# Halo rows as column strips, interleaved feature groups and re-timed DMA in a hybrid decoder layer on eight cores

## The chip, the cores and the metric

The program runs on all 8 cores of one Trainium2 chip (two dies of four cores); every core executes the same instructions on its own part of the data. In the profiles of this kernel TensorE does the matrix products, VectorE, ScalarE and GpSimd the rest of the arithmetic, and SyncE only issues DMAs. The metric is the time of the slowest core in microseconds (us). Such a program has a second, slower state in some executions, in which the cores of one die show a lower granted TensorE clock (0.91 on one die and 0.98 on the other in an execution of 1988.9 us, for example); only executions in the fast state are compared here. A profile covers one execution, with all eight cores; where I give "the median of the cores", it is over the eight cores of one profiled execution.

## The reference, cut to what matters

```python
def mixer(xn, conf_buf, lru_buf, h0, p, reset_first):
    proj = xn @ p['w_in']                                  # 2048 -> a_val, a_gate, b_x, b_gate (1024 each)
    a_val, a_gate, b_x, b_gate = jnp.split(proj, ...)
    u = a_val * jax.nn.sigmoid(a_gate)
    ca, new_conf = causal_dwconv(u, conf_buf, ...)         # depthwise, 31 taps
    ca = silu(layer_norm(ca, ...))
    xc, new_lru = causal_dwconv(b_x, lru_buf, ...)         # depthwise, 4 taps
    h, h_last = rglru(xc, h0, ...)                         # gates, then a linear scan over time
    cb = h * gelu(b_gate)
    return jnp.concatenate([ca, cb], axis=-1) @ p['w_out'], ...

def conv_ffn(xn, buf, p):
    up = xn @ p['w_up']                                    # 2048 -> 12288
    upc, new_buf = causal_dwconv(up, buf, ...)             # depthwise, 3 taps
    g, v = jnp.split(upc, 2, axis=-1)
    return (gelu(g) * v) @ p['w_down'], new_buf            # 6144 -> 2048

def layer(x, ...):
    x = x + rms_norm(mixer(rms_norm(x, ...))[0], ...)
    return x + rms_norm(conv_ffn(rms_norm(x, ...))[0], ...)
```

There are 4 prompts of 2048 tokens and 128 short sequences of 8 tokens. A core takes half a prompt (1024 tokens) and 16 short sequences (128 tokens): 9 tiles of 128 rows. A core with a second half also computes what the scan and the convolutions need of the first half, among that two rows just ahead of its first tile, which only the 3-tap convolution of the channel mixer reads. These two rows are the **halo tile**.

## The kernel before

The kernel writes one list of instructions per engine and derives the semaphore waits from what each reads and writes; a buffer placed over an older one waits for the older one's last readers. Each engine executes its list in order, and a DMA is issued from an engine's list, so a DMA that has to wait holds whatever stands behind it on that engine. `load("sp", ...)` is a DMA issued from SyncE, `load("pool", ...)` one from GpSimd. TensorE's products land in the banks of the PSUM memory (`PS`), from which ScalarE or VectorE copies them out.

Its stages in order are: normalise and transpose 17 row tiles, input projection and 31-tap convolutions (to about 430 us); the recurrent group with the layer norm (to about 580); output projection and the two norms, tile by tile (to about 750); up projection and down projection, in two halves of the hidden features (to about 1906); the last outputs. In the lines of the profile, xnp is a transposed row tile of the first half, which the input projection reads; xcpb the result of the 4-tap convolution of the first half, which the gates read; wab and wxb the gates' weights; ge one half of the up projection's result; hm the product that the down projection reads; a number behind a name only tells buffers apart. These parts matter for the argument:

```python
# diagonals for the 31-tap convolution as a matmul: built on GpSimd
def conv_prep(j):
    load("pool", r_w, T[f"ubf{j % 2}"][:, 1056:1536], st_conf_d[:, j]...)
    S.op("pool", lambda e: e.tensor_tensor(dg[:], identb..., vecs..., ALU.mult), ...)

# five transfers just ahead of the convolutions, in the stretch in which row tiles are loaded
load("pool", r_su, T["wab"][:], wa_d, ...);  load("pool", r_su, T["wxb"][:], wx_d, ...)
load("sp", r_su, T["slruc"][:], ...);        load("sp", r_su, T["slruh"][:], ...)
load("sp", r_out, s_conf_d[:, :, 0:22, :], st_conf_d[:, :, 8:30, :], [], [])

# output projection: ten tiles, the first with the 2 halo rows
tiles = [(1022, 2, 0, None)] + [(1024 + 128 * t, 128, 2 + 128 * t, 128 * t) for t in range(9)]

# down projection, second half of the hidden features (g == 1): 36 items (feature group fg, tile)
items = [(fg, tt_) for fg in range(4) for tt_ in range(9)]
def down_load(i):
    load("sp", r_ld, T["prv"][:, i % 3, :], f_scr[rows, ...], ...)   # first half's partial sum
    if fg == 3:
        load("sp", r_x, T[f"hh{tt_ % 3}"][:], h_scr[rows, :], ...)   # h, for the residual
for i, (fg, tt_) in enumerate(items):
    down_load(i + 2)
    down_mm(g, fg, tt_, b)                                           # 24 matmuls
    tt(f, out, prv, ALU.add);  act(Square, accum);  tt(f, f, grow3, ALU.mult)
    if fg == 3:                                                      # tile complete
        ...                                                          # reciprocal root of the sum of squares
        stt(hh, f3, r, hh, ...)                                      # hh = f * r * gain + h
        load("sp", r_out, y_d[rows, :], hh[:], [kh_], [])            # output
```

Of the kernel before, what the change touches and what calls it, by code (L numbers as in the profile page):

```python
# [55 lines left out]
class Sched:  # L56
# [135 lines left out]
    "xnp0": 0, "x2_0": 0, "xna0": 15872, "xna1": 34816, "catA5": 8192, "xn20": 10528, "wp9": 0, "ca6": 53760, "f36":  # L192
    4096, "xcb0": 0, "catB2": 58400, "ca1": 58400, "ca5": 63040, "f35": 10240, "hm1": 28992, "hm16": 31296, "xs2":
    53760, "grow2": 28992, "ca3": 67680, "hh2": 16384, "wp6": 33600, "catB4": 60736, "catA6": 63072, "ones": 72320,
    "catB7": 37184, "og1": 4096, "x2_1": 39520, "wp11": 37696, "xcpbZ": 72832, "wo03": 65408, "catB0": 73600,
    "catB3": 75936, "wu1": 78272, "wp10": 41792, "wu2": 82368, "hh0": 45888, "ve0": 45888, "grow3": 54080, "A3":
    86464, "catA3": 86464, "t3_1": 10528, "xnp1": 91104, "ca7": 106976, "flags": 111616, "hm13": 62272, "xcpZ":
    111648, "wo10": 47712, "th": 72832, "catA2": 88800, "wu4": 115616, "grow1": 78272, "wo12": 91136, "wo01":
    111648, "wo11": 99328, "wo02": 119840, "ubf1": 111648, "ge1": 50656, "ca4": 119712, "hm6": 64576, "xt1": 63040,
    "hm2": 66880, "wo13": 128032, "catA4": 136224, "wu0": 124352, "xs0": 106976, "prv": 69184, "ffnf": 69184,  # L200
    "hm15": 82240, "wp3": 107520, "ge0": 55424, "gbg1": 138560, "wu3": 128448, "f34": 75328, "slruc": 143200, "wxb":
    144736, "hm23": 84544, "hm9": 86848, "hm5": 89152, "fl": 24576, "hm18": 91456, "xcb1": 146784, "gbg2": 2464,
    "hm19": 93760, "wp5": 96064, "ca2": 132544, "hm0": 100160, "t2_0": 149248, "hm8": 102464, "xs1": 119712, "f30":
    111648, "hm4": 104768, "p1Z": 137184, "catA1": 154176, "catB1": 156512, "wo00": 158848, "hm20": 117792, "xn21":
    167040, "xcpb": 141152, "catA0": 185504, "wp2": 138560, "slruh": 167040, "us1": 77568, "f31": 120096, "catB5":
    187840, "catA7": 190176, "hh1": 126240, "xt2": 132544, "xs2_1": 143200, "dj": 134432, "hm22": 135456, "xc0":
    91136, "ov1": 111648, "hstf": 167552, "xs2_0": 147296, "wp8": 151392, "hm12": 155488, "xt0": 146784, "og0":
    120096, "ht": 192512, "hm11": 157792, "t2_1": 168096, "wp0": 200704, "f37": 142656, "bxp": 146784, "diag1":
    154976, "btl": 173024, "wu5": 162912, "p1": 150784, "t3_0": 173120, "hm7": 160096, "bxe": 96064, "t1_1": 178048,
    "ov0": 124832, "hm21": 162400, "p3Z": 154752, "wab": 182976, "hP": 185024, "hm17": 164704, "grow0": 167552,  # L210
    "wp7": 185504, "ssf": 28672, "wp1": 204800, "us0": 114976, "xcp": 168096, "catB6": 55904, "xc1": 192512, "tiny":
    208896, "t1_0": 197440, "ca0": 178048, "hm14": 189600, "sq": 185056, "ve1": 129568, "wp4": 191904, "bxpZ":
    158720, "gbg0": 202368, "ubf0": 189792, "cv": 209152, "f33": 167008, "f32": 173152, "hm10": 196000, "p3":
    173120, "dstg": 142656, "identb": 209280, "A3b": 193120, "vecs": 209536, "rs": 101024, "diag0": 197760, "f38":
    179296, "lrucf": 207008, "mu": 187840, "hm3": 198304,
# [3 lines left out]
def build_program():  # L219
# [22 lines left out]
    st_ffn_d = din("st_ffn", [128, 96, 32])  # L242

# [5 lines left out]
    ffn_d = dout("ffn", [128, 96, 34])  # L249
# [4 lines left out]
    with ExitStack() as es:  # L254
# [29 lines left out]
            ("grow1", [D], F_, 17, 20), ("grow2", [D], F_, 17, 20),  # L284
            ("ht", [D], F_, 18.2, 20), 
            ("grow3", [D], F_, 22.9, 24),
            ("ffnf", [96, 34], F_, 20, 22.9), 
# [8 lines left out]
        for i in range(2):  # L296
            BUFS += [(f"diag{i}", [31, 128], B_, 0, 8), (f"ubf{i}", [1664], B_, 0, 8), (f"us{i}", [158], F_, 0, 8.2)]
            BUFS += [(f"xc{i}", [1232], F_, 8.6 + i * 1.4, 17 + i), (f"xcb{i}", [1232], B_, 8.6 + i * 1.4, 17 + i)]
            BUFS += [(f"{t}_{i}", [1232], F_, 10 + i, 18 + 0.4 * i) for t in ("t1", "t2", "t3")]
            BUFS += [(f"x2_{i}", [D], F_, 17, 20), (f"xs2_{i}", [D], B_, 18.2, 20.5)]  # L300
            BUFS += [(f"ge{i}", [1186], F_, 20, 22.9), (f"ve{i}", [1186], F_, 20, 22.9)]
            BUFS += [(f"og{i}", [1184], F_, 20, 22.9), (f"ov{i}", [1184], F_, 20, 22.9)]
# [4 lines left out]
        for i in range(24):  # L307
            BUFS += [(f"hm{i}", [1152], B_, 20, 24)]
# [9 lines left out]
        for i in range(12):  # L318
            BUFS += [(f"wp{i}", [2048], B_, 19 if i < 4 else 20, 24)]
# [195 lines left out]
        def conv_prep(j):  # L515
            load("pool", r_w, T[f"ubf{j % 2}"][:, 1056:1536], st_conf_d[:, j].rearrange("p t s -> p (t s)"),
                 [], [(f"ubf{j % 2}", "o")])
            dg = T[f"diag{j % 2}"]
            S.op("pool", lambda e: e.tensor_tensor(
                dg[:], identb[:].unsqueeze(1).broadcast_to([128, 31, 128]),  # L520
                vecs[:, V_CW + 31 * j:V_CW + 31 * j + 31].unsqueeze(2).broadcast_to([128, 31, 128]), ALU.mult),
                ["identb", "vecs"], [(f"diag{j % 2}",)])
# [243 lines left out]
        load_w(4, after=[("xt2",)])  # L766
        p0_norm(0)
# [25 lines left out]
        conv_prep(0)  # L793
        conv_prep(1)
# [11 lines left out]
        load("pool", r_su, T["wab"][:], wa_d, [], ["wab"])  # L806
        load("pool", r_su, T["wxb"][:], wx_d, [], ["wxb"])
        load("sp", r_su, T["slruc"][:], st_lruc_d, [], ["slruc"])
        load("sp", r_su, T["slruh"][:], st_h_d.rearrange("p j s o -> p j (s o)"), [], ["slruh"])
        load("sp", r_out, s_conf_d[:, :, 0:22, :], st_conf_d[:, :, 8:30, :], [], [])  # L810
# [25 lines left out]
        for j in range(2, 8):  # L836
            conv_prep(j)
            i = j - 1
            bg = triple()
# [72 lines left out]
        tiles = [(1022, 2, 0, None)] + [(1024 + 128 * t, 128, 2 + 128 * t, 128 * t) for t in range(9)]  # L912
        NT = len(tiles)

        def p2_load(ti):
            r0, M, a0, hr = tiles[ti]
            load("sp", r_x, T[f"x2_{ti % 2}"][0:M, :], xall[r0:r0 + M, :], [], [(f"x2_{ti % 2}",)])

        def cat(k, a0, M):
            return T[f"catA{k}" if k < 8 else f"catB{k - 8}"][:, a0:a0 + M]  # L920
# [3 lines left out]

        def p2_mm(ti, k0, k1, half=None):
            r0, M, a0, hr = tiles[ti]
            b0 = 4 * (ti % 2)
            for fg in range(4):
                if fg == 2 and half is not None:
                    half()  # L930
                for k in range(k0, k1):
                    mm(PS[0:M, 512 * (b0 + fg):512 * (b0 + fg) + 512], cat(k, a0, M), T[f"wo{k // 8}{fg}"][:, k % 8, :],
                       k == 0, k == 15, cat_keys(k) + [(f"wo{k // 8}{fg}",)], PK(b0 + fg), skip=True)

        def p2_begin():
            load("sp", r_su, T["grow1"][:], grows_d[1:2, :].partition_broadcast(128), [], ["grow1"])
            load("sp", r_su, T["grow2"][:], grows_d[2:3, :].partition_broadcast(128), [], ["grow2"])
            p2_load(0)
            p2_load(1)

# [38 lines left out]
        for k0, k1 in ((0, 8), (8, 14)):  # L979
            for ti in range(2):  # L980
# [16 lines left out]
        def p2_norm(ti, between=None):  # L997
            r0, M, a0, hr = tiles[ti]
            b0 = 4 * (ti % 2)
            x2, xs, ht = T[f"x2_{ti % 2}"], T[f"xs2_{ti % 2}"], T["ht"]  # L1000
            kx, ks = (f"x2_{ti % 2}",), (f"xs2_{ti % 2}",)
            o = PS[0:M, 512 * b0:512 * b0 + 2048]
            c = tiny[0:M, 16 + 8 * (ti % 2):24 + 8 * (ti % 2)]
            kt = lambda n: ("tiny", "p2", ti % 2, n)
            act(xs[0:M, 0:1024], o[:, 0:1024], AF.Square, PK(b0, 2), [ks, kt(0)], accum=c[:, 0:1])
            if between is not None:
                between()
            act(xs[0:M, 1024:2048], o[:, 1024:2048], AF.Square, PK(b0 + 2, 2), [ks, kt(1)], accum=c[:, 1:2])
# [3 lines left out]
            stt(ht[0:M, :], o, c[:, 3:4], T["grow1"][0:M, :], ALU.mult, ALU.mult, PK(b0, 4) + [kt(3), "grow1"], ["ht"])  # L1012
            tt(x2[0:M, :], x2[0:M, :], ht[0:M, :], ALU.add, [kx, "ht"], [kx])
            if hr is not None:
                load("sp", r_st, h_scr[hr:hr + 128, :], x2[:], [kx], [("h_scr", hr)])
            act(xs[0:M, :], x2[0:M, :], AF.Square, [kx], [ks, kt(4)], accum=c[:, 4:5])
            act(c[:, 5:6], c[:, 4:5], AF.Ln, [kt(4)], [kt(5)], scale=1.0 / D, bias=EPS)
            act(c[:, 6:7], c[:, 5:6], AF.Exp, [kt(5)], [kt(6)], scale=-0.5)
            if hr is None:
                ts(c[:, 6:7], c[:, 6:7], flags[0:M, 0:1], None, ALU.mult, None, [kt(6), "flags"], [kt(6)])  # L1020
            stt(xs[0:M, :], x2[0:M, :], c[:, 6:7], T["grow2"][0:M, :], ALU.mult, ALU.mult, [kx, kt(6), "grow2"], [ks])

        def p2_turn(ti, b0):
            r0, M, a0, hr = tiles[ti]
            xs, ks = T[f"xs2_{ti % 2}"], (f"xs2_{ti % 2}",)
            for kh in range(2):
                b = b0 + kh
                pb = PS[:, 512 * b:512 * b + 512].bitcast(BF16)
                for j in range(8):
                    k = 8 * kh + j  # L1030
                    S.op("pe", lambda e, pb=pb, j=j, k=k: e.transpose(pb[:, 128 * j:128 * j + M],  # L1031
                                                                      xs[0:M, 128 * k:128 * k + 128], identb[0:M, 0:M]),
                         [ks, "identb"], PK(b))
                pv = pb.rearrange("p (j t) -> p j t", t=128)
                evac("dve" if kh == 0 else "act", T[f"xn2{kh}"][:, :, a0:a0 + M], pv[:, :, 0:M], PK(b), [(f"xn2{kh}", ti)])
# [3 lines left out]
        p2_mm(1, 15, 16)  # L1039
        p2_load(2)  # L1040
        p2_norm(1)
# [272 lines left out]
```

## Time and profile before

The fast executions of the first measurement took 1946.76 and 1948.91 us; the others (2071.99 and 3807.41) were in the slow state, and they are why the median is 2072. The table cuts the profiled execution of the kernel before at points that are easy to find in any trace (first start of an instruction on a tile), each as the median of the cores, with their spread.

| Stretch | us before | over the cores |
|---|---|---|
| start to the last gate sigmoid of the convolution stage (ScalarE on p1Z) | 430.4 | 427.0 to 433.8 |
| to the issue of the last output weight ("recurrent stage") | 147.7 | 147.0 to 147.9 |
| to the first normalising multiply of the output projection | 46.2 | 45.8 to 47.2 |
| to the last of them ("output projection") | 126.3 | 125.7 to 126.4 |
| to TensorE's end (up and down projection) | 1152.4 | 1149.0 to 1155.4 |
| TensorE's end to the kernel's end ("the end") | 36.7 | 35.2 to 38.2 |

A stretch is read on its own: a stage in which TensorE is 100% busy is shortened, at the same clock, only by less TensorE work, and one in which it stands by whatever it stands for. The lines of the profile that carry this are in the prediction. Two more views of the kernel before are needed later: what VectorE waits for in the last 80 us, and the longest wait of SyncE's list from 1780 us on. Columns of the waits: total us, times, longest.

```profile
DVE sb_hh_96 L364 <- DMA sb_hh_96<-h_scr: 7.9, 2, 4.0
DVE sb_hh_92 L364 <- DMA sb_hh_92<-h_scr: 5.8, 2, 3.8
```

### The profile page before, as it was taken

The numbers are of one execution on the slowest core, as the hardware profiler recorded it, in microseconds if no ns is written. First come the engines' busy times: TensorE is split into PE (matmuls) and PEld (weight loads), VectorE is DVE, ScalarE is ACT, GpSimd is POOL, SyncE is SP. The second block draws the span as 40 slices with busy tenths as digits, with TensorE's granted clock in tenths as the row PEclk, the third lists the DMA queues.
The fourth block names the chain that finished last, engine by engine and source line by source line (L and its number), as shares of the span: only waits on it lengthen the run. The fifth ranks groups of instructions, "written<-read, shape, count | busy, mean of one in ns | idle before, by whom it ended". The sixth has DMA issues, their size and how long they took to land.

```text
span 1944.6 us, 33585 instructions; the slowest of 8 cores (1931.5 to 1944.6 us)
## 1 busy us (share of the span) xinstructions
PE 1773.5 (91%) x10412; PEld 916.8 (47%) x10412; DVE 1012.2 (52%) x968; ACT 567.2 (29%) x1009; POOL 182.6 (9%) x247
## 2 busy tenths in 40 slices
PE   2868999999986999799999989999999999989992
PEld 2744565554442444355555544444555555544440
DVE  5534655557883554666666650001666666642243
ACT  3633234347882433222222211111222222211110
POOL 3002221101221001000000000000000000000000
PEclk9979999999998999899999999999999999999996
DMA  8672322313268435743344325556344334445566
GB/s 195 201 165 38 51 38 39 53 33 63 44 133 155 152 130 143 134 72 66 66 67 74 67 55 110 124 114 119 67 72 70 66 66 68 74 121 115 119 206 233
DMA packets 53127, 193.48 MB, mean 99 GB/s; under 512 B 6994, under 2 KB 10578, under 8 KB 44498
## 3 DMA queue, kind: packets, MB, share of 16 engines
q0 software_dynamic: 29232, 106.41, 32.6%
q1 hardware_dynamic: 23716, 84.92, 13.1%
q8 instruction: 84, 1.38, 0.3%
q14 instruction: 95, 0.78, 0.1%
HBM read 266.79 MB, written 32.35 MB: 154 GB/s over the span
## 4 chain that ended last, share of the span: by engine, by line
PE 83%; DMA 9%; DVE 4%; ACT 2%; issue 2%; SPq 0%; DVEq 0%; ACTq 0%; POOL 0%; POOLq 0%
PE ps L370 82%; DMA sb_xt_90<-xall 2%; DMA sb_wo_201<-w_out 2%; DMA sb_ffnf<-st_ffn 1%; DMA y<-sb_hh_96 1%; DMA y<-sb_hh_92 1%; DVE sb_xs_95 L364 1%; DMA sb_xt_94<-xall 1%; PE ps L463 1%; DMA y<-sb_hh_88 0%; ACT L337 0%; PE ps L1031 0%; DVE sb_btl L343 0%; DMA sb_hh_96<-h_scr 0%; SPq L373 0%
## 5 line engine op out<-in xcount | busy, mean ns | idle before, releaser
L343 DVE COPY sb_ve_108<-ps 128x1026 f32<-128x1026 f32 (+1 forms) x48 | 36.4, 800 | 306.5 <-PE ps L370 306.5
L343 DVE COPY sb_ve_122<-ps 128x1026 f32<-128x1026 f32 (+1 forms) x48 | 36.4, 800 | 108.7 <-PE ps L370 108.7
L364 DVE SCALAR_TENSOR_TENSOR sb_ov_110<-sb_ve_108,sb_vecs,sb_ov_110 128x1184 f32<-128x1184 f32 x48 | 69.7, 1451 | 5.3 <-DVE sb_ov_110 L361 0.5
L364 DVE SCALAR_TENSOR_TENSOR sb_og_109<-sb_ge_107,sb_vecs,sb_og_109 128x1184 f32<-128x1184 f32 x48 | 69.7, 1451 | 5.3 <-DVE sb_og_109 L361 0.5
L364 DVE SCALAR_TENSOR_TENSOR sb_og_123<-sb_ge_121,sb_vecs,sb_og_123 128x1184 f32<-128x1184 f32 x48 | 69.7, 1452 | 5.0
L364 DVE SCALAR_TENSOR_TENSOR sb_ov_124<-sb_ve_122,sb_vecs,sb_ov_124 128x1184 f32<-128x1184 f32 x48 | 69.7, 1451 | 5.0
L335 ACT COPY sb_dstg<-ps 128x512 f32<-128x512 f32 x36 | 21.1, 586 | 167.0 <-PE ps L370 167.0
L370 PE MATMUL ps<-sb_ubf_112,sb_diag_111 128*128 128x342 bf16 (+1 forms) x496 | 63.9, 290 | 0.0
L370 PE MATMUL ps<-sb_ubf_98,sb_diag_97 128*128 128x342 bf16 (+1 forms) x496 | 62.2, 286 | 0.0
L335 ACT COPY sb_ffnf<-sb_ve_122 128x32 f32<-128x32 f32 (+1 forms) x48 | 7.5, 205 | 178.4 <-DVE sb_ve_122 L343 178.4
L335 ACT COPY sb_ffnf<-sb_ve_108 128x32 f32<-128x32 f32 (+1 forms) x48 | 7.6, 204 | 175.3 <-DVE sb_ve_108 L343 175.2
L370 PEld LDWEIGHTS ps<-sb_ubf_112,sb_diag_111 128*128 128x128 bf16 x496 | 43.8, 99 | 19.5
L337 ACT ACTIVATE sb_og_123<-sb_og_123 128x1184 f32<-128x1184 f32 x24 | 28.6, 1191 | 82.4 <-DVE sb_og_123 L364 82.4
L337 ACT ACT_TABLE_LOAD x37 | 47.5, 1283 | 17.5 <-PE ps L370 7.8
L370 PEld LDWEIGHTS ps<-sb_ubf_98,sb_diag_97 128*128 128x128 bf16 x496 | 43.1, 97 | 18.5
L337 ACT ACTIVATE sb_og_109<-sb_og_109 128x1184 f32<-128x1184 f32 x24 | 28.6, 1190 | 79.5 <-DVE sb_og_109 L364 79.5
L370 PE MATMUL ps<-sb_xn_127,sb_wp_206 128*128 128x512 bf16 (+1 forms) x192 | 36.8, 335 | 11.8 <-ACT sb_ge_121 L335 11.8
L343 DVE COPY sb_btl<-sb_bxp 128x3 f32<-128x3 f32 x7 | 36.4, 5204 | 16.2 <-ACT sb_bxp L335 16.2
L335 ACT COPY sb_ge_107<-ps 128x1026 f32<-128x1026 f32 (+1 forms) x48 | 31.4, 705 | 34.8 <-PE ps L370 34.8
L370 PE MATMUL ps<-sb_xna_125,sb_wu_182 128*128 128x512 bf16 (+2 forms) x184 | 33.9, 330 | 6.8 <-DMA sb_wu_182<-w_in 6.8
L335 ACT COPY sb_ge_121<-ps 128x1026 f32<-128x1026 f32 (+1 forms) x48 | 31.4, 707 | 26.7 <-PE ps L370 26.7
L370 PE MATMUL ps<-sb_xn_130,sb_wp_206 128*128 128x512 bf16 (+1 forms) x192 | 36.4, 333 | 0.0
(654 smaller groups left out, 4135.7 us busy)
## 6 DMA issues: line engine op xcount, KB each, us to landing
f_scr<-sb_dstg SPq DMA_DIRECT2D x36, 256.0 KB, 3.4
sb_prv<-f_scr SPq DMA_DIRECT2D x36, 256.0 KB, 4.5
sb_xt_86<-xall SPq DMA_DIRECT2D x6, 1024.0 KB, 7.5
sb_xt_90<-xall SPq DMA_DIRECT2D x6, 1024.0 KB, 8.6
sb_xt_94<-xall SPq DMA_DIRECT2D x5, 1024.0 KB, 11.8
sb_x_1_119<-xall SPq DMA_DIRECT2D x5, 1024.0 KB, 5.4
h_scr<-sb_x_1_119 SPq DMA_DIRECT2D x5, 1024.0 KB, 3.9
sb_wp_202<-w_up POOLq DMA_DIRECT2D x8, 512.0 KB, 6.8
```

The lines of the kernel that those rows point to most:

```text
L335: S.op("act", lambda e: e.copy(out=out, in_=in_), reads, writes)
L337: S.op("act", lambda e: e.activation(out=out, in_=in_, func=func, scale=scale, bias=bias), reads, writes)
L343: S.op("dve", lambda e: e.tensor_copy(out, in_), reads, writes)
L364: S.op("dve", lambda e: e.scalar_tensor_tensor(out, a, s, b, op0, op1), reads, writes)
L370: S.op("pe", lambda e: e.matmul(out, lhsT, rhs, start=start, stop=stop, skip_group_check=skip), reads, writes)
L463: S.op("pe", lambda e, pb=pb, j=j, k=k: e.transpose(pb[:, 128 * j:128 * j + 128], xs[:, 128 * k:128 * k + 128], identb[:]), [ks, "identb"] ...
```

## The change

Its intent is to take waits of TensorE away at six places. The diff, cut to its core (left out are the new addresses of all buffers, the renamed state tensors, the exchanged order of the first two tiles of the output projection, the small operations on the halo rows, and the reloads of h for tiles 0 to 2, which now leave at item 18 of 36):

```diff
+        def conv_diag(j):                                    # now on VectorE
+            tt(T[f"diag{j % 2}"][:], identb..., vecs..., ALU.mult, ...)
@@ the five transfers go from ahead of the convolutions into their loop
+            if j == 2:    load wab, wxb
+            elif j == 4:  load slruc, slruh
+            elif j == 5:  load s_conf
@@ output projection: 9 full tiles; the halo rows in four 32-column strips of the array
-        tiles = [(1022, 2, 0, None)] + [...]
+        def halo_mm(b):
+            for k in range(16):
+                for fg in range(4):
+                    mm(PS[32 * fg:32 * fg + 32, 512 * b:512 * b + 512], cat(k, 0, 32), T[f"wo{k // 8}{fg}"][:, k % 8, :], ...)
+            act(zh[:], PS[:, 512 * b:512 * b + 512], ...)
@@ grow1, grow2, x tiles wait for the last output weight
+            last = [("wo13",)]
+            load("sp", r_su, T["grow1"][:], ..., last, ["grow1"])
@@ state of the up projection: one contiguous tile, loaded at the end of the last tile
+                load("sp", r_su, T["ffo"][:], st_ffn_d, [], [("ffo", "old")])
@@ down projection: 23 of 24 products of three tiles ahead of the last hidden group
+                if i == 0:
+                    for t in range(3):
+                        down_mm(g, fg, t, (b + t) % 8, 0, 23)
@@ last two feature groups interleaved, output in two pieces, reload right behind it
+            if g == 1:
+                items = items[:24]
+                for t in range(3):
+                    items += [(3, t), (2, 6 + t)]
+                items += [(3, t) for t in range(3, 9)]
-                load("sp", r_out, y_d[rows, :], hh[:], [kh_], [])
+                load("sp", r_out, y_d[rows, 0:1536], hh[:, 0:1536], [(kh_, 0)], [])
+                load("sp", r_out, y_d[rows, 1536:2048], hh[:, 1536:2048], [(kh_, 1)], [])
+                if tt_ < 6:
+                    hh_load(tt_ + 3)
```

## The prediction

> **What bounds the kernel now.** I read the clocks of the cores first: spans 1931.5 to 1944.6 us, clocks 0.963 to 0.966 on both dies, so the profiled execution is a fast one (its time was 1946.3 us; 1946.8 is the lowest of the timed ones, and the median of 2072 holds slow ones). All that follows is about fast executions. Next, the busy shares on the page and the stretches of time:
>
> ```profile
> PE 1773.5 (91%) x10412; PEld 916.8 (47%) x10412; DVE 1012.2 (52%) x968; ACT 567.2 (29%) x1009; POOL 182.6 (9%) x247
> ```
> ```profile
> 98.00:132.00 34.00, 15.12 (x155) 11.61 (x154) 8.76 (x8) 9.33 (x15) 0.00 (x0) 0.77 0.93 204
> ...
> 580.00:614.00 34.00, 22.25 (x81) 7.44 (x78) 16.26 (x20) 12.92 (x13) 6.29 (x11) 0.79 1.01 193
> ...
> 646.00:760.00 114.00, 114.00 (x638) 55.71 (x637) 62.76 (x41) 46.50 (x89) 0.70 (x2) 1.00 0.36 137
> 760.00:796.00 36.00, 23.43 (x166) 12.68 (x164) 11.53 (x10) 7.79 (x17) 5.63 (x11) 0.90 1.00 191
> ...
> 1865.00:1945.00 80.00, 41.44 (x192) 18.58 (x190) 35.82 (x45) 11.43 (x37) 0.00 (x0) 0.79 0.64 223
> ```
>
> Columns after the stretch: PE, PEld, DVE, ACT, POOL busy, granted clock, DMA share, GB/s. TensorE is the bound: 91% of the span, and 100% in the long stretches. Only two things can shorten the time: less TensorE work, and fewer of its 171 us of gaps. Three gaps lie where the DMA share is 0.93 to 1.01, and the last where TensorE is done and outputs still leave. TensorE's own waits name them:
>
> ```profile
> PE ps L463 <- DVE sb_xnp_126 L343: 18.9, 1, 18.9
> ...
> PE ps L370 <- ACT sb_ge_121 L335: 11.8, 1, 11.8
> PE ps L370 <- DVE sb_hm_170 L355: 10.1, 2, 5.9
> ```
>
> The landing times (last column) say what stood behind two of them and behind the output weights:
>
> ```profile
> sb_ffnf<-st_ffn SPq DMA_DIRECT2D x1, 1536.0 KB, 28.9
> s_conf<-st_conf SPq DMA_DIRECT2D x1, 1408.0 KB, 23.8
> ...
> sb_wo_201<-w_out POOLq DMA_DIRECT2D x1, 1024.0 KB, 32.3
> ```
>
> And the group tables show two costs of building diagonals on GpSimd: 6.8 us each there, and a VectorE copy of three elements that takes 5.2 us on average:
>
> ```profile
> L519 POOL TENSOR_TENSOR sb_diag_97<-sb_identb,sb_vecs 128x3968 bf16<-128x3968 bf16 x4 | 27.4, 6848 | 0.0
> ```
> ```profile
> L343 DVE COPY sb_btl<-sb_bxp 128x3 f32<-128x3 f32 x7 | 36.4, 5204 | 16.2 <-ACT sb_bxp L335 16.2
> ```
>
> **What the Trainium skill says.** (1) "TensorE: Matmul & The Clock Gate", Part 3: matmuls with at most 32 stationary columns in different column strips run together; it gives 2.38x for three strips with 512 moving columns. "TensorEngine Tiling (Array Packing)", Key Properties, adds that a change of tiling mode drains the engine. The trace before has only 2-column matmuls in one strip: 0.216 us each, no cheaper than full ones, so the gain is not tested. (2) "GPSIMD Engine Reference", Specifications: its SBUF interfaces are shared with VectorE, with contention when VectorE has two SBUF inputs or a 2-port mode. Agrees: the copy above is 0.17 us when no diagonal is being built, 7.2 us in the median, and one 2048-column multiply took 14.5 us against 2.35. (3) "DMA: Bandwidth & Descriptors", Queues, rings and completion order: an engine takes turns between queues by packets. Agrees: one 1 MB row tile lands in 5.0 us in calm and in 12.6 beside two weight loads.
>
> **Part by part.** Two rates from the DMA part of the page: the SP queue moved 84.92 MB in 13.1% of 1944.6 us, so 3.0 us per MB; the POOL queue 106.41 MB in 32.6%, so 6.0 us per MB written (it casts). An output weight of 1 MB is thus 6 us, and the last ones landed 6.2 apart.
>
> 1. Front. Eight diagonals move to VectorE. One costs 3968 elements at the rate of a 1232-element multiply (1.44 us), 4.5 us; two precede the first evacuations and delay them some 4 us, but TensorE then waits for the third weight (landing at 41.2) anyway. Gone: the 14.5 us multiply, worth only 1.6 us since the load behind it also waits for weights landing at 43.7. More comes from the DMAs moved out of 96 to 98 us: the DRAM copy of s_conf, slruc, slruh, wab, wxb. The row tile queued behind them took 26.6 us to land, and TensorE stood 18.9. Left there: four weights (24 us) and four row tiles (12 us) from 88 us on; with the SP queue getting a third of the engines while both run, tiles 13 to 16 land near 106, 115, 124 and 127, and leave stalls of about 0.4, 3.5 and 3.7. The second convolution should end at 137 instead of 153: 15.5 us. Behind it the 6.3 us wait for xcpb (behind the slow copy) becomes some 4.5 for wab, now loaded late; two waits of 1.3 and 2.8 may shrink. Sum **18**. From 212 to 432 us TensorE is full and nothing changes.
>
> 2. Output weights. grow1, grow2 and the x tiles now wait for the last one. Before, two loads were slowed from 562 us by grow1 and grow2, the next by x. Alone, the four issued at 579 to 582 land at 579.1+2+4x6.2 = 606 instead of 613.9: **8**. The norm needs grow1 14 us after the last weight; it lands after 5 to 7.
>
> 3. Halo tile. Out: 64 matmuls of 0.216, 13.8 us, and 0.9 of transposes. It ran partly in the wait for weights, but now a full tile takes that place, so one of eight tiles in the full stretch goes. In: 64 strip matmuls; at threefold overlap (estimate from the skill's 2.38 for three) 4.6 us, 0.25 of transposes, and 1.5 because strip and fourth group share a PSUM bank, whose copy stands in ScalarE's order behind the previous norm. **8.5**. Its small VectorE ops (some 6 us in all) lie in a stretch where VectorE is 55% busy.
>
> 4. State of the up-projection. The scattered load of 28.9 us becomes contiguous, and is issued at the end of the last tile instead of 9.6 us later, behind a store. At a third of the engines it lands about 17 to 19 us later, just when ScalarE wants it. The 11.8 us gap goes, and with it 1.7 of half-speed matmuls after it (0.43 instead of 0.22 us): **13**.
>
> 5. Up to down. hm23 comes 11.0 us after the last up matmul, both times. Three tiles of 23 matmuls are 14.9 us, so the wait is covered. Gaps 5.9+4.2, 1.5 for a bank still being emptied, and 1.6+1.7 of half speed: **14.5**.
>
> 6. End. TensorE finishes at 1906.3 and the kernel 38 us later. The chain of waits shows why:
>
> ```profile
> 1896.79 8.92 DMA y<-sb_hh_88
> ...
> 1906.31 8.69 DMA y<-sb_hh_92
> ...
> 1915.58 9.85 DMA y<-sb_hh_96
> 1925.55 6.59 DMA sb_hh_96<-h_scr
> ```
>
> Output, then reload of its buffer, in one queue: 9.3 us per tile against 5.2 of TensorE. Interleaving gives the first three finished tiles 10.4 us each. Going through the queue with 2 us latency and 3.0 per MB, reloads 3 to 6 come in time, reload 7 makes a little delay, reload 8 lands about 6 us after TensorE's end; its output lands 9 later, and 3.5 us of closing as before: 18.7 instead of 38. **19**.
>
> Sum 18+8+8.5+13+14.5+19 = 81. 1946-81 = 1865 us.
>
> **The rivals.** (a) Strips do not overlap: 64 x 0.216 again, 1874. For it: the narrow matmuls seen were as slow as full ones. Against: they lay in one strip. (b) DMA stays the bound where its share is near 1: moved transfers collide again, tiles 13 to 16 come late, and SP still waits for each output before the next, so parts 1 and 6 give half: about 1883. For it: share 0.93 at the front. Against: 11 us of transfers leave that stretch. (c) VectorE becomes the bound in the convolutions: it was 53% busy from 212 to 432 and trades seven stalls of some 5 us for six builds of 4.5, so no. (d) The new placement of all buffers makes a load wait for a late reader; no row shows it, up to 10 us. (e) A denser TensorE gets a lower clock: the clock was 0.99 to 1.00 in the full stretches, so I expect none in fast executions.
>
> **Range and chances.** (a) and (b) together give 1892; a better front (no stalls, 5 more) and end (8 more) with the small waits in part 1 gone give about 1845. So 1843 to 1890. Faster by 2% means below 1907, which needs half of the sum: parts 4 and 5 and one other, so 0.96; within 2% 0.035; slower 0.005.
>
> **What would show it.** TensorE's waits should no longer list hm or a 12 us wait for ge; the xnp wait should be under 8 in sum, w_out's last landing some 8 us earlier relative to its issue; 64 strip matmuls within 6 us; diagonals near 4.5 us on VectorE and no 3-element copy above 1; less than 22 us between the last matmul and the end. Wrong would be: a new wait of TensorE over 5 us for wab, a diagonal or the first up-projection weights, or a lower clock in all cores.

## More of the kernel before

```profile
SPq L178 <- DMA y<-sb_hh_96: 17.4, 2, 9.0
```

The reloads of h come late there, and they come late since each waits in SyncE's list until the output that left from the same buffer has landed: for the three buffers together the list stood 43.3 us.

## The result, and the profile after

The changed kernel took 1877.67, 1879.36, 1879.37 and 1879.92 us: 69 us less than the fast executions of the kernel before. The ratio of the two is 0.965, with a 95% interval of 0.963 to 0.967; ratios here are the mean time of one kernel's fast runs over that of the other's in the same rounds, so not quite the ratio of the medians that I quote. It is faster by 3.5%. Executions in which one die ran at a lower clock are left out of the means.

Cut at the same points, the changed kernel's profiled execution shows where the time went:

| Stretch | before | after | gain | predicted (part) |
|---|---|---|---|---|
| convolution stage | 430.4 | 405.1 | 25.3 | 18 (1) |
| recurrent stage | 147.7 | 152.5 | -4.8 | 0 |
| to the first normalising multiply | 46.2 | 38.8 | 7.4 | 8 (2) |
| output projection | 126.3 | 121.3 | 5.0 | 8.5 (3) |
| up and down projection | 1152.4 | 1122.1 | 30.3 | 27.5 (4, 5) |
| the end | 36.7 | 32.3 | 4.4 | 19 (6) |
| span | 1939.8 | 1871.5 | 68.3 | 81 |

(The medians of the stretches add up to 67.6; a median of sums is not the sum of medians. The cut between parts 2 and 3 is soft, since the kernel before normalises its halo tile first.)

The stretches of time that answer to those of the prediction, now at the changed kernel's positions. Columns: PE, PEld, DVE, ACT, POOL busy, granted clock, DMA share, GB/s.

```profile
95.42:129.42 34.00, 28.73 (x248) 20.81 (x247) 17.08 (x14) 16.99 (x26) 0.00 (x0) 0.90 0.65 170
561.00:588.00 27.00, 18.38 (x80) 7.62 (x79) 15.78 (x19) 11.64 (x11) 3.77 (x6) 0.94 0.90 154
...
718.00:754.00 36.00, 35.03 (x230) 18.37 (x228) 20.44 (x19) 12.28 (x26) 7.92 (x14) 1.00 0.98 193
1787.00:1876.00 89.00, 57.20 (x266) 25.73 (x263) 39.16 (x51) 13.61 (x43) 0.00 (x0) 0.85 0.60 204
```

In the first, TensorE now works 28.7 of 34 us where it had 15.1, and the DMA share went from 0.93 to 0.65. In the third the gap of the up projection's state is gone, although the DMAs are as full as before. In the last TensorE has more to do, but the stretch has become no shorter. What TensorE waited for, in the whole run:

```profile
PE ps L467 <- DVE sb_xnp_131 L347: 5.3, 1, 5.3
...
PE ps L374 <- DVE sb_xn_135 L347: 3.2, 1, 3.2
...
PE ps L374 <- DMA sb_wab<-wa: 1.3, 1, 1.3
...
PE ps L374 <- ACT sb_ge_112 L339: 0.3, 1, 0.3
```

The 18.9 us for xnp have become 5.3, the 11.8 for ge 0.3, and hm is not in the list at all. The wait for xn in the middle is new. The end is another picture. First what VectorE, then what SyncE's list waited for from 1787 us on, and then pieces of the chain of waits (start, duration, what):

```profile
DVE sb_fl L359 <- DMA sb_prv<-f_scr: 13.2, 4, 5.4
```
```profile
SPq L178 <- DMA y<-sb_hh_97: 14.3, 4, 8.4
SPq L178 <- DMA y<-sb_hh_101: 13.2, 4, 7.2
...
SPq L178 <- DMA y<-sb_hh_93: 9.6, 4, 4.9
```
```profile
1820.54 6.53 DMA sb_prv<-f_scr
...
1832.85 10.54 DMA y<-sb_hh_97
...
1844.87 8.33 DMA y<-sb_hh_101
...
1853.79 6.45 DMA sb_prv<-f_scr
```

On this core TensorE's last matmul ended at 1844.2. The reload of tile 7's h was issued at 1843.5, when the output of its buffer had landed after 10.5 us; the prv load of a tile stands right behind a reload and left 0.5 us later; so it went on, and the last prv was issued at 1853.8 and landed at 1860.3. VectorE waits for prv, whose own buffer had been free since 1840 us: it only stands in the wrong place of the list. The Trainium skill ("DMA: Bandwidth & Descriptors", Anatomy of one DMA — SWDGE (gpsimd) path) says that a DMA's wait for a semaphore happens on the issuing engine ahead of its dispatch; this trace agrees, with 37.1 us (14.3 + 13.2 + 9.6) that SyncE's list stood for landing outputs.

### The profile page after: what moved, and what is told of

Read it like the earlier page. It is cut to its first block, busy times and chain, and to the rows that moved or that the text cites. A ratio compares the mean times of both kernels' runs of the same rounds, so it can differ in the third digit from the quotient of the medians.

```text
span 1875.9 us, 33549 instructions; the slowest of 8 cores (1863.6 to 1875.9 us)
## 1 busy us (share of the span) xinstructions
PE 1757.1 (94%) x10400; PEld 913.3 (49%) x10400; DVE 988.9 (53%) x994; ACT 564.0 (30%) x1007; POOL 126.9 (7%) x239
## 3 DMA queue, kind: packets, MB, share of 16 engines
q1 hardware_dynamic: 24848, 85.69, 13.5%
## 4 chain that ended last, share of the span: by engine, by line
PE 85%; DMA 8%; ACT 2%; DVE 2%; issue 2%; SPq 0%; POOL 0%; DVEq 0%; ACTq 0%; POOLq 0%
PE ps L374 85%; DMA sb_xt_99<-xall 2%; DMA sb_wo_206<-w_out 1%; DMA sb_prv<-f_scr 1%; DMA sb_xt_95<-xall 1%; DMA y<-sb_hh_101 1%; DMA sb_wu_187<-w_in 1%; DMA y<-sb_hh_97 1%; ACT L341 0%; PE ps L467 0%; PE ps L1043 0%; DMA sb_wab<-wa 0%; SPq L377 0%; DVE sb_fl L359 0%; DVE sb_ht L368 0%
## 5 line engine op out<-in xcount | busy, mean ns | idle before, releaser
L339 ACT COPY sb_ffo<-sb_ve_127 128x32 f32<-128x32 f32 x24 | 5.3, 219 | 182.6 <-DVE sb_ve_127 L347 182.6
L339 ACT COPY sb_ffo<-sb_ve_113 128x32 f32<-128x32 f32 x24 | 5.3, 220 | 175.5 <-DVE sb_ve_113 L347 175.5
L341 ACT ACT_TABLE_LOAD x37 | 47.5, 1283 | 17.9 <-PE ps L374 7.0
L374 PE MATMUL ps<-sb_xn_132,sb_wp_207 128*128 128x512 bf16 (+1 forms) x192 | 35.1, 325 | 0.5 <-DVE sb_xn_132 L347 0.5
L374 PE MATMUL ps<-sb_xn_132,sb_wp_209 128*128 128x512 bf16 (+1 forms) x192 | 35.1, 325 | 0.3 <-ACT sb_ge_112 L339 0.3
L374 PE MATMUL ps<-sb_xn_135,sb_wp_207 128*128 128x512 bf16 (+1 forms) x192 | 35.1, 325 | 0.1
## 6 DMA issues: line engine op xcount, KB each, us to landing
sb_xt_95<-xall SPq DMA_DIRECT2D x6, 1024.0 KB, 10.4
```

The costliest lines, as they stand in the source:

```text
L339: S.op("act", lambda e: e.copy(out=out, in_=in_), reads, writes)
L341: S.op("act", lambda e: e.activation(out=out, in_=in_, func=func, scale=scale, bias=bias), reads, writes)
L374: S.op("pe", lambda e: e.matmul(out, lhsT, rhs, start=start, stop=stop, skip_group_check=skip), reads, writes)
```

## The experiments

Each is the changed kernel with one edit, unless it says otherwise. All gave correct results. In nine profiled executions whose end was not edited, the stretch from TensorE's end to the kernel's was 28.7 to 32.3 us, with 31.1 in the middle; so a difference of 2 us in it means little, and 31.1 is the figure to compare with.

### The end: the reload in its queue

**Reloads issued from GpSimd.**

```diff
-                load("sp", r_x, T[f"hh{t % 3}"][:], h_scr[...])
+                load("pool", r_hh, T[f"hh{t % 3}"][:], h_scr[...])
```

> The changed kernel with one edit: the nine reloads of h (hh) are issued from GpSimd's queue instead of SyncE's, with their own semaphores. Theory A (the order of one queue): in the changed kernel each reload waits in SyncE's queue for the output of its buffer to land, and the prv load and the next output stand behind it, so VectorE waits 13.2+5.4+4 us for prv; then this run should end 6 to 10 us earlier than the changed kernel (1879 us), some 1870 us, and VectorE's wait for prv should fall from 13.2 us to under 3, with hh the later wait. Theory B (DMA bandwidth at the end): the same bytes move through the same 16 engines, so within 2 us of the changed kernel, about 1878, with prv landing as late as now.

Measured: fast runs 1872.5 to 1874.5 us, ratio to the kernel before 0.962; the end took 24.0 us in the median of the cores, where the unedited one has 31.1. VectorE's wait for prv is gone, and one of 9.1 us for h is the later wait, as theory A said. (The text above adds up 13.2, 5.4 and 4, which are the total, the longest and the number of the same four waits; the sum is 13.2.) The end is 7 us shorter and the time some 6 us, with the same bytes moved, which speaks against bandwidth. A second queue might also change how the DMA engines share the bytes; the next run, and the one with the last reloads freed, stay in SyncE's list.

**Reloads one group later.**

```diff
-                if tt_ < 6:
-                    hh_load(tt_ + 3)
+                pend.append(tt_ + 3)          # issued in the next item, after its down_load
```

> The changed kernel with each reload of h issued one group later in SyncE's queue, so that one prv load and one output pass ahead of it. Theory A: the wait moves from prv to hh, since the last reload still waits for the output two groups before; the gain is small, 0 to 5 us (1874 to 1879), and VectorE's waits of over 3 us at the end name hh instead of prv. Theory B (bandwidth): no change of time and none in what VectorE waits for.

Measured: 1870.0 and 1874.9 us (ratio 0.961); the end took 25.8 us. A mere change of order in one list took 5 us off the end, and VectorE's longer waits now name the reload (13.2 us in three) and not prv (3.0), as theory A said.

**Only prv moved to GpSimd's queue.**

```diff
-                load("sp", r_ld, T["prv"][:, i % 3, :], f_scr[...])
+                load("pool", r_ld, T["prv"][:, i % 3, :], f_scr[...])
```

> The changed kernel with only the prv loads moved from SyncE's queue to GpSimd's. Theory A as sharpened (prv is what comes late, because it stands behind a reload that waits for an output to land): VectorE's waits for prv of 13.2 us fall under 2, but the reloads still follow the outputs one by one, so hh becomes the wait; end 22 to 27 us after TensorE instead of 32.3, the time 5 to 10 us less: 1869 to 1874. Theory B (bandwidth): 32 us after TensorE as before, 1879.

This missed: 1873.9 to 1881.8 us, in the middle 1879.2, and the end took 29.6 us, within the spread of the unedited kernel. What VectorE waited for at the end, and SyncE's list:

```profile
DVE sb_hh L368 <- DMA sb_hh<-h_scr: 15.6, 3, 6.2
```
```profile
SPq L178 <- DMA y<-sb_hh: 44.0, 11, 8.5
```

The wait for prv is gone and one for the reload has taken its place, 15.6 us for 13.2 (18.4 with the two rows of waits for prv not shown above). So prv was where the wait showed, and the reload behind its output is where it comes from.

**Last reloads freed of the outputs.** Tiles 6 and 7 are reloaded into weight buffers that are free by then, tile 8 into tile 3's buffer after the outputs of tile 5. Four weight buffers change their addresses for it.

```diff
+            def hh_of(t):
+                return {6: "hhA", 7: "hhB", 8: "hh0"}.get(t, f"hh{t % 3}")   # hhA, hhB lie on wp2, wp3 and wp4, wp5
+                if g == 1 and i == 30:
+                    hh_load(6); hh_load(7)
-                if tt_ < 6:
+                if tt_ < 3:
                     hh_load(tt_ + 3)
+                if tt_ == 5:
+                    hh_load(8)
```

> The changed kernel with the last three reloads freed of the outputs: tiles 6 and 7 are reloaded into the four weight buffers of feature group 2, which are free when its last product is done, and tile 8 into the buffer of tile 3, issued after the outputs of tile 5, when tile 3's have landed. Theory A: nothing in the queue stands behind an output any more; TensorE still ends near 1844 us, the last output leaves 6 us later and the kernel ends some 18 us after TensorE (31.7 in the changed kernel): 1865 us, 12 to 15 us less. Theory B (bandwidth): 1877, since the bytes are the same.

Measured: 1867.4 and 1870.2 us (the other two executions were slow, so there is no interval); the end took 19.9 us. The 11 us are a little under the 12 to 15 expected: the reloads of tiles 3 to 5 still stand behind outputs, and VectorE still waits 12.6 us for prv.

**Order and pieces.** Three runs: plain order instead of the interleaving; plain order with the late reloads of above; and the output in one piece again.

```diff
@@ plain order
-                items = items[:24]
-                for t in range(3): items += [(3, t), (2, 6 + t)]
-                items += [(3, t) for t in range(3, 9)]
@@ one piece
-                load("sp", r_out, y_d[rows, 0:1536], ...); load("sp", r_out, y_d[rows, 1536:2048], ...)
+                load("sp", r_out, y_d[rows, :], hh[:], [(kh_, 0), (kh_, 1)], [])
```

> The changed kernel with its interleaving of the last two feature groups undone (all of group 2, then tiles 0 to 8 of group 3); outputs stay in two pieces and the first three reloads stay early. Theory A: tile by tile at 5.2 us of TensorE against an output and a reload of some 10 us per buffer of three, the reloads fall behind earlier: 4 to 8 us more than the changed kernel, 1884 to 1888, and VectorE waits longer for prv or hh. If the interleaving buys nothing because the queue is the limit from tile 4 on either way, the time is within 2 us of 1879.

> The changed kernel with plain order of the last groups and the reloads one group later in the queue, which is the order of the kernel before, but with outputs in two pieces. If the place of the reload right behind its output is what the changed kernel gave back (plain order, reload at once: 46.1 us from TensorE's end to the kernel's; interleaved, at once: 32.3; interleaved, later: 25.8), this fourth corner is 36 to 40 us, near the 36.7 of the kernel before. If the two pieces are what costs, it is over 42.

> The changed kernel with each tile's output in one piece again. If the place of the reload is the cause, the piece counts little: from TensorE's end to the kernel's within 3 us of 32.3. If the small second piece slows the queue, 27 or less; if the pieces help, over 35.

| TensorE's end to the kernel's end, us | reload right behind its output | one group later |
|---|---|---|
| interleaved | 31.1 (the changed kernel) | 25.8 |
| plain order | 46.1 | 42.6 |

The times were 1892.2 us (ratio 0.971) for plain order, more than the 1884 to 1888 expected, 1892.1 for plain order with late reloads, 1876.7 for one piece. Interleaving is worth 15 to 17 us of the end, at either place of the reloads. The later place is worth 5.3 us with the interleaving, where the time shows it too; in plain order the 3.5 us are not shown, since the cores spread from 43.7 to 49.2 and from 38.8 to 47.2 and the times are equal. With the interleaving, one piece ended after 28.0 us, where the unedited kernel on the same chip took 28.7, so there the pieces do nothing that can be seen. The fourth corner missed its expectation: 42.6 us and not the 36 to 40 expected if it were the kernel before. The changed kernel's end in plain order thus costs 9.4 us more than the end of the kernel before; the place of the reload makes 3.5 of them by these two executions, which is not shown, and the rest stays open. One rival was not tested: two pieces in plain order. On the slowest core of each, one reload follows the last after 10.1 to 11.5 us in the fourth corner and after 9.3 to 10.4 in the kernel before, whose outputs leave in one piece.

### The front: diagonals and transfers

```diff
@@ diagonals on GpSimd
-            tt(T[f"diag{j % 2}"][:], identb..., vecs..., ALU.mult, ...)
+            S.op("pool", lambda e: e.tensor_tensor(dg[:], identb..., vecs..., ALU.mult), ...)
@@ transfers at their old place: the five loads back behind done_w("v", 1), out of the loop over j
```

> The changed kernel with the diagonals built on GpSimd again, at the changed kernel's places. In the kernel before the conv stage ended at 430.4 us (median of the cores), in the changed one at 405.1, 25.3 earlier, where I had predicted 18: 15.5 from the DMAs moved, 1.6 from the diagonals, the rest small. If the DMAs carry it, this run ends the stage 1 to 6 us later than the changed kernel (406 to 411) and the time is about 1880 to 1885; if VectorE freed of its blocked copies and multiplies carries it, 10 us or more later (over 415).

> The changed kernel with the five transfers (two gate weights, two states, the copy of the convolution state) issued at their old place ahead of the convolutions. If they carry the front, the conv stage ends 12 to 18 us later than in the changed kernel, 417 to 423, TensorE's wait for xnp is back at over 12 us, and the time is about 1893. If the diagonals carry it, under 6 us later. The small wait of TensorE for wab (1.3 us in the changed kernel) should be gone.

> The changed kernel with both front parts undone (diagonals on GpSimd, the five transfers ahead of the convolutions). Alone they ended the conv stage at 419.9 and 418.2 us against 405.1. If their costs add, 431 to 435 here, close to the 430.4 of the kernel before; if each hides the other in part (both delay the same second convolution), 421 to 427.

| convolution stage ends at, us (median of the cores) | transfers moved | transfers at the old place |
|---|---|---|
| diagonals on VectorE | 405.1 | 418.2 |
| diagonals on GpSimd | 419.9 | 431.4 |

The kernel before stands at 430.4. The times were 1891.9, 1889.4 and 1903.2 us (ratios 0.971, 0.971 and 0.977; the last, with an interval of 0.973 to 0.982, is unclear against a gain of 2%). The transfers give 13.1 us, the diagonals 14.8, and together undone they give 26.3: the two parts are nearly additive, and they are the whole gain of this stage. For the transfers, TensorE's waits in the run that has them at the old place say why, and it is what was predicted:

```profile
PE ps L467 <- DVE sb_xnp L347: 19.3, 1, 19.3
```

For the diagonals on GpSimd two waits of TensorE come back which the changed kernel does not have, and the copy of three elements explains them. First the waits, then the copy (min, median, max in ns) in that run, then the same copy in the changed kernel:

```profile
PE ps L374 <- DVE sb_xcpb L347: 6.4, 1, 6.4
...
PE ps L374 <- ACT sb_sq L341: 2.8, 1, 2.8
```
```profile
L347 DVE COPY sb_btl<-sb_bxp x7: 169/7192/7195, 148.0 to 380.1; 128x3 f32<-128x3 f32 x7
```
```profile
L347 DVE COPY sb_btl<-sb_bxp x7: 169/301/303, 145.8 to 366.5; 128x3 f32<-128x3 f32 x7
```

A diagonal takes 6.84 us on GpSimd here, and the copy that meets it takes 7.19; a diagonal takes 4.29 us on VectorE, and the copy 0.30. Of the 14.8 us, 3.1 are there before the first convolution starts (93.9 instead of 90.8 us), the wait for xcpb adds some 5 (6.4 instead of 1.3 for the gate weights), the wait for sq 2.8. The remaining 4 or so are slower matmuls: from the first convolution to the end of the stage TensorE is busy 308.2 us, where the changed kernel has 304.4 (medians of the cores). Most of that lies behind the two waits: on core 0 the granted clock is 0.59 in the 5 us behind the first of them and 0.79 in the 8 us behind the second, and 1.00 in between.

### Halo strips

```diff
-            for k in range(16):
-                for fg in range(4):
+            for fg in range(4):
+                for k in range(16):
                     mm(PS[32 * fg:32 * fg + 32, ...], cat(k, 0, 32), ...)
```

> The changed kernel with the 64 matmuls of the halo tile in the order strip by strip, so that each strip's 16 follow one another, and not round the four strips. Theory A (strips overlap only when neighbours lie in different strips): the 64 take 13.8 us instead of 3.6, the stretch of the output projection from the first to the last normalised tile grows by 10 us from 121.3 to 131, and the time to about 1889. Theory B (they overlap whatever the order, or the gain of this part came from somewhere else): within 2 us of the changed kernel.

Measured: 1884.8 us (ratio 0.968), under the 1889 expected, and 128.9 us for the output projection where the changed kernel has 121.3. The timelines tell why it is 7.6 and not 10. First the changed kernel, round the strips (start, duration), then strip by strip:

```profile
614.25 0.39 PE L374 MATMUL ps<-sb_wo_199,sb_catA_136 128*32 128x512 bf16 x1
614.25 0.39 PE L374 MATMUL ps<-sb_wo_200,sb_catA_136 128*32 128x512 bf16 x1
...
617.51 0.38 PE L374 MATMUL ps<-sb_wo_206,sb_catB_151 128*32 128x512 bf16 x1
```
```profile
611.75 1.90 PE L374 MATMUL ps<-sb_wo,sb_catA 128*32 128x512 bf16 x8
613.49 1.24 PE L374 MATMUL ps<-sb_wo,sb_catB 128*32 128x512 bf16 x5
614.35 0.39 PE L374 MATMUL ps<-sb_wo,sb_catA 128*32 128x512 bf16 x1
614.56 0.38 PE L374 MATMUL ps<-sb_wo,sb_catB 128*32 128x512 bf16 x1
614.58 0.38 PE L374 MATMUL ps<-sb_wo,sb_catA 128*32 128x512 bf16 x1
...
621.30 1.89 PE L374 MATMUL ps<-sb_wo,sb_catB 128*32 128x512 bf16 x8
```

Round the strips, four matmuls start within 0.01 us and all 64 take from 614.25 to some 617.8. Strip by strip they take 11.4 us, and only around a change of strip do two run together: the last three of strip one (catB) with the first three of strip two (catA). So the overlap is real and needs neighbours in different strips; that theory held, and its rival fell.

### Placement

```diff
-    "xc1": 53248, ... "t1_1": 23584
+    "xc1": 23584, ... "t1_1": 53248
```

The recurrent stage had become 4.8 us longer, on all eight cores, though the change does not touch its instructions. ScalarE's waits in that stage of the changed kernel name the cause of a part: it waits for VectorE's copy of a scan's last value (hP), which it does not use.

```profile
ACT sb_xc_119 L341 <- DVE sb_hP L347: 3.1, 1, 3.1
```

> The changed kernel with the addresses of two buffers of equal size exchanged (xc1 and t1_1). In the changed kernel xc1 lies on p3Z and bxpZ, which VectorE reads until 432 us, so ScalarE's first write of xc1 waits 3.1 us and TensorE behind it 1.8. Theory A (placement, the fourth rival of the prediction): the stage from the last sigmoid of the convolutions to the issue of the last output weight, 152.5 us in the median of the changed kernel's cores and 147.7 in the kernel before, falls by 2 to 4 us to 148.5 to 150.5, the wait of ScalarE for hP is gone, and the time falls by about as much, to some 1876. Theory B: the stage is longer because TensorE's granted clock falls more often there; then it stays within 1 us of 152.5.

Measured: 1875.5 us (ratio 0.963), the stage 150.3 us, and the wait gone. So some 2 of the 4.8 us are the placement. The median alone would not show it, since one run without this edit (reloads one group later) also has 150.4 where the others have 151.6 to 152.7; that the waits are gone does: TensorE's waits in the stage are 19 us on most cores, what they were before, and 20 to 23 in the changed kernel. The remaining 2.6 us are the same 735 matmuls at a lower granted clock, on one core 132.8 us busy at 0.92 where the kernel before had 129.7 at 0.95. Why the clock is lower there stays open.

### The wait for the output weights, and the three tiles ahead

```diff
@@ no wait
-            last = [("wo13",)]
+            last = []
@@ no lead
-                if i == 0:
-                    for t in range(3):
-                        down_mm(g, fg, t, (b + t) % 8, 0, 23)
```

> The changed kernel without the wait that holds grow1, grow2 and the x tiles behind the last output weight. My prediction gave that wait 8 us. From the issue of the last output weight to the first normalised tile it is 38.8 us in the changed kernel and 46.2 in the one before, so if the wait carries it, 5 to 8 us more here (44 to 47), and the time 1884 to 1887; if the reordering of the two tiles carries it, within 2 us of 38.8.

> The changed kernel without the three-tile lead of the down projection: each tile's 24 products stand together again. My prediction gave the lead 14.5 us over both groups of hidden features. From the last normalised tile to TensorE's end it is 1122.1 us in the changed kernel and 1152.4 in the one before; if the prediction's split is right, 13 to 16 us more here (1135 to 1138), TensorE's wait for hm is back at some 10 us in sum, and the time is 1892 to 1895; the other 14 to 17 us of this stretch then belong to the state of the up projection (predicted 13).

Without the wait, 49.9 us pass from the issue of the last output weight to the first normalising multiply, 11.1 more than with it and 3.7 more than in the kernel before; the time was 1889.7 us (ratio 0.968). TensorE's wait for output weights is 17.9 us in it, 8.6 in the changed kernel. Taken away, the wait costs more than the 7.4 us seen and the 5 to 8 expected; a likely reason, not tested, is that it also keeps the new loads for the halo rows out of that stretch.

Without the lead, up and down projection take 1139.5 us, 17.4 more; TensorE waits for hm again:

```profile
PE ps L374 <- DVE sb_hm L359: 11.8, 2, 5.9
```

The fast runs were 1895.1, 1895.5 and 1913.7 us (ratio 0.974, interval 0.967 to 0.981, so a gain of 2% over the kernel before is unclear in this one); in the profiled one two cores of a die were 1.5% low in clock, but this stretch agrees on all eight (1139.0 to 1140.0). The other 12.9 us of the stretch (30.3 less 17.4) are left for the state of the up projection, which no run took away alone; TensorE's wait for ge, 11.8 us before and 0.3 now, fits it.

### The changed kernel again, and a version that beats both

> The changed kernel once more, unedited, as reference on the same chip: 1876 to 1882 us in the fast state, conv stage ending at 405, 32 us from TensorE's end to the kernel's.

On the same chip as the last runs it took 1876.5 and 1877.4 us (ratio 0.964), with the convolution stage ending at 404.8 and 28.7 us of end.

The last version joins four edits: the exchanged addresses; the freed reloads; prv on GpSimd's queue; and the four transposes of the halo rows one tile earlier, so that no matmul stands behind them. (In the changed kernel their bank is emptied behind VectorE's 2.35 us multiply, and tile 8 needs it: the wait for xn of 3.2 us above.)

```diff
-            half = {3: ..., 8: lambda: halo_turn(p2_bank(8) + 3)}.get(ti)
+            half = {3: ...}.get(ti)
+            # after the transposes of tile 6, ahead of tile 8's matmuls:
+                if ti == 7:
+                    halo_turn(p2_bank(8) + 1)
```

> A version meant to beat both: the changed kernel with the exchanged addresses (the earlier run took 2.2 us from its stage), the transposes of the halo tile one tile earlier so that no bank of tile 8 stands behind VectorE's 2.35 us multiply (TensorE waited 3.2 us there), the last reloads freed of the outputs as in the run that did so (end 19.9 us after TensorE instead of 32.3), and the prv loads on GpSimd's queue, so that they no longer stand behind an output at all. Theory A (the order of SyncE's queue makes the end): VectorE takes the last group under 2 us after TensorE's end, and the kernel ends 14 to 18 us after TensorE; sum of gains 2.2 + 3.2 + 15, so 1857 to 1862 us. If something else holds the end at 20 us after TensorE: 1863 to 1867.

Measured: 1859.03, 1859.14 and 1859.25 us, ratio to the kernel before 0.952 (0.948 to 0.956): 20 us less than the changed kernel and some 90 less than the kernel before. Stretch by stretch, the recurrent stage took 149.8 us, the output projection 117.8, the end 17.5, with VectorE taking the last group 1.9 us after TensorE's end. The list of SyncE shows the order that does it:

```profile
1835.95 0.33 SPq L378 DMA_DIRECT2D sb_hh<-h_scr  x1
1836.36 0.92 SPq L378 DMA_DIRECT2D y<-sb_hhA  x2
1838.56 0.99 SPq L378 DMA_DIRECT2D y<-sb_hhB  x2
1847.81 0.99 SPq L378 DMA_DIRECT2D y<-sb_hh  x2
```

The last reload leaves before TensorE has finished, and only outputs stand behind it. One wait is left: VectorE stands 4.4 us for that last reload. On this core outputs took up to 18.7 us to land near the end, longer than in the changed kernel, and yet the end is shorter: what counts is what stands behind an output. With prv moved as well, the end is 17.5 us for the 19.9 of the freed reloads alone, little more than such stretches differ from run to run, and prv moved alone saved next to nothing: it takes away a wait that another one hides.

## Why the prediction was right or wrong, point by point

The direction and the order of size held, and the time lies in the range given. The point was 14 us too low, and two terms of the sum of 81 were badly mis-sized, in opposite directions; that they cancel in part is luck. (The sum itself is rounded: as written, the six parts come to 18.9, 7.9, 8.4, 13.5, 14.9 and 19.3, so 83.)

**The end (predicted 19, measured 4.4, or 5.6 against the middle of nine executions): wrong, and the larger miss.** The step that failed is "Going through the queue with 2 us latency and 3.0 per MB, reloads 3 to 6 come in time, reload 7 makes a little delay, reload 8 lands about 6 us after TensorE's end". Two things are wrong in it. An output took 8.0 to 10.6 us from issue to landing in the last 12 us before TensorE's end and after it (the very last 3.3), and not the 5 of the queue model, although the prediction's own fence of the kernel before shows 8.7 to 9.9. And I followed only the reloads, while the list in which they stand also carries prv and the next output: each reload now stands right behind the output it waits for. On the profiled core reload 8, predicted to have landed 6 us after TensorE's end, was issued 9.1 and landed 15.4 us after it, and the last prv stood behind it. With the last reloads freed of the outputs the end took 19.9 us, near the 18.7 predicted. The interleaving itself is worth the 15 to 17 us that I had hoped for, but from a start that was 9.4 us worse; what makes these 9.4 is open (the place of the reload perhaps 3.5).

**The front (predicted 18, measured 25.3): wrong in one term.** The transfers were put at 15.5 us and measured 13.1. The diagonals were put at "worth only 1.6 us", with small waits that "may shrink", and measured 14.8. I had the 7.2 us copies before me, but took the wait for xcpb of 6.3 as exchanged for 4.5 of wab, and it was exchanged for 1.3; I counted the 2.8 of sq as nothing, and it vanished; I set the start of the convolutions aside, where 3 us came from; and I did not count the matmuls that run at a lower clock behind each wait, another 4.

**The recurrent stage (predicted unchanged, measured 4.8 longer).** Rival (d) named the mechanism, a new placement that waits for a late reader, at up to 10 us; it is some 2. Rival (e), a lower clock, I had expected to be nothing; it fits the other 2.6, without a cause shown.

**Output weights (8, measured 7.4) and lead and state (14.5 and 13, measured 17.4 and 12.9): right,** and the mechanism is shown for the first two by taking them away (11.1 us more without the wait, 17.4 without the lead). For the state, 12.9 is what is left over; it landed 11.0 us after its issue, where I expected 17 to 19.

**Halo tile (8.5, measured 5.0): right in the mechanism, with one wait not foreseen.** The strips overlap better than estimated (3.6 us for the predicted 4.6), so rival (a) is out. Against that stands the 3.2 us wait behind the transposes; with them moved, the stretch shrinks by 8.5 us (126.3 to 117.8).

**Rival (b)** said that SyncE would wait for each output before the next and put the time at 1883. Its half about the end was right, its half about the front wrong. **Rival (c)** did not come: TensorE lost nothing to VectorE's diagonals in the convolution loop.

## What to carry to other kernels

A queue is a list in order: place a DMA that must wait for another to land behind everything that need not, or give it another buffer, and follow every entry of the list, also the ones that wait for nothing. A cost that two engines make together is not seen in the row of either; the copy of three elements at 7.2 us was the row to take seriously, and all that stood behind it. After moving buffers, look for waits in stages that the change does not touch.

## What the Trainium skill lacked or had wrong

- "TensorE: Matmul & The Clock Gate", Part 3, Measured speedup vs the span model: it has 2.38x for three column strips of 512 columns and none for four. Here four strips took 3.6 us for 64 matmuls that cost 13.8 one by one (64 x 0.216), 3.9x.
- The same part lacks what the order does: strip by strip, the same 64 took 11.4 us, with an overlap of about three matmuls at each change of strip.
- "TensorEngine Tiling (Array Packing)", Key Properties: it says that a change of tiling mode drains the engine, but not what that costs. Little here: the first strip matmul began 0.31 us after the last full one, where 0.216 is the pace.
- "DMA: Bandwidth & Descriptors", Anatomy of one DMA: it says that the wait is on the issuing engine, but not what follows: everything behind it on that engine waits too. Here SyncE's list stood 37.1 us for landing outputs at the end, and VectorE stood 13.2 us for loads of prv that were behind them.
